# The last sequence's value pages, moved from the end of the paged stage into the prompt's attention

## The chip, the cores and the metric

The kernel runs on one core of one Trainium2 chip. The metric is device microseconds for one execution; the time of the kernel before is the median of three runs. A core has the engines PE (matmul), DVE, ACT and POOL, an SP queue that issues most of the transfers, and 16 DMA engines that move data between HBM and the on-chip memory SBUF. Matmul results land in PSUM.

## What is computed

The reference is one inference step of a trunk of two layers for a prompt of 1024 tokens (with 16 meta tokens ahead of it) and for eight running sequences that each add one token. Layer 0 mixes by gated linear attention, layer 1 by differential attention; each is followed by an MLP and normalisations. The change concerns layer 1. There the prompt attends to itself, and each of the eight new tokens attends to its own 4096 past tokens, whose keys and values lie in 32 pages of 128 tokens, found through a page table:

```python
def diff_core(q, k, v, q_pos, k_pos, lam):
    s = jnp.einsum('bqhmd,bkhmd->bhmqk', q, k).astype(F32) * (DIFF_DH ** -0.5)
    s = jnp.where(k_pos[None, :] <= q_pos[:, None], s, -jnp.inf)
    p = jax.nn.softmax(s, axis=-1)
    a = p[:, :, 0] - lam * p[:, :, 1]
    return jnp.einsum('bhqk,bkhe->bqhe', a, v.astype(F32))
...
    k_past = cache_k[page_table].reshape(B, past, DIFF_HEADS, 2, DIFF_DH)
    v_past = cache_v[page_table].reshape(B, past, DIFF_HEADS, DIFF_DV)
```

All is 32-bit floating point. There are 8 heads; each has two score maps (m = 0, 1), of which the second is subtracted with a learned factor. A page is 128 tokens x 1024 numbers, 512 KB.

## The kernel before, in words

The kernel is one program for one core. The order of instructions on each engine is fixed at build time by a list scheduler, which follows the order of the code and a priority; at run time each engine takes its list in order and waits on semaphores.

The stages that matter here, in order:

**The paged stage.** The generator `decode()` (L855) runs beside layer 0's output, its MLP, and layer 1's projection. For the sequences b = 0 to 7 it loads 32 key pages each, multiplies each with the query (L796, three of four on DVE and one on POOL) and sums per head (L797). `soft()` (L800) makes the softmax weights of a sequence, 33 x 16 numbers on each partition. One sequence later, mixed with the keys of the next, the value pages are loaded (`v_load`, L822) and multiplied (`v_pages`, L832): a page takes four matmuls (L837) with 16 columns of weights each, which write to four groups of partitions of one PSUM bank; all 33 pages (32 and the new token's own value row) add into that bank, `acc`, from the small ring `smt` of two banks. `v_end` (L842) copies the sum out and transposes it to `oT`, which the samples need only in layer 1's output stage. The page loads run in a background priority, behind everything else. In the loop over `range(NS + 1)` the ninth pass has no keys left: it is the eighth sequence's (b = 7) values alone, one page behind the other. Page tiles come from the pool `pgp`, of 8 buffers of 4 KB a partition. A page's load reads its number from the page table into a register on SP (`value_load`), and each such read is issued after the fourth load before it.

**Layer 1's projection** (L1091 on): 12 units of 256 columns, matmuls L186 to L188 with a left operand XH, XL and split weights. A unit's result is copied to a tile `qo` (L1104) and stored (L1121). After unit 8, `prep_qk(0, ...)` prepares head 0 of the attention. After the stage the pools of the paged stage are closed (`de.close()`), and attention's own pools are opened on the right side of SBUF, upon bytes that the closed pools had; a tile waits for the tiles that had its bytes before.

**The prompt's attention** (loop at L1240): 8 heads of 8 tiles of 128 queries. `prep(h)` (L1170) loads a head's keys and queries (L1059, L1060), the meta tokens' keys (L1061), the meta values `vm` (L1175) and the values `vx` (L1176) on SP's queue, transposes keys and queries on PE (L1068 to L1078), splits them in two (L182, L183), and moves halves between partitions by nine transfers on POOL's queue (L1082 to L1088). It is called one head ahead. `tile_` (L1179) makes the scores of a tile on PE (L1192, L1193), brings them to SBUF with mask and running minimum on DVE (L1196), exponentiates on ACT (L1198), combines the two maps on DVE (L1202), transposes on PE (L1211), copies on ACT (L1213) and multiplies with the values on PE (L1216). The products of four tiles gather in one bank `po` from the ring `smt`; then ACT copies them out (L1251) and squares them in place (L1252), and DVE sums the squares (L1253).

After it come layer 1's output matrix (`w_out`), with the samples' part `samples()`, and the second MLP.

Of the kernel before, what the change touches and what calls it, by code (L numbers as in the profile page):

```python
# [11 lines left out]
F32 = mybir.dt.float32  # L12
F32R = mybir.dt.float32r
U8 = mybir.dt.uint8
I32 = mybir.dt.int32
AF = mybir.ActivationFunctionType
ALU = mybir.AluOpType
# [9 lines left out]
NS = 8  # L27
# [83 lines left out]
def hybrid_step(ctx, tc, A, dbg=None, upto=9):  # L111
# [20 lines left out]
    def smt():  # L132
        return sm.tile([P, 512], F32, name="smt")
# [602 lines left out]
    @contextmanager  # L736
    def background():
        at = tc.cur_priority
        tc.cur_priority = bg_at[0]
        yield  # L740
        bg_at[0] = tc.cur_priority
        tc.cur_priority = at

    ptab = dp.tile([NS, NPG], I32, name="ptab")
    dma(ptab, A["page_table"])

    lamv = kp.tile([P, 2], F32, name="lamv")
# [9 lines left out]

    gathers = []

    def page(cache, b, n):  # L760

        with tc.issue_after(gathers[-4]) if len(gathers) > 3 else nullcontext():
            r = nc.sync.value_load(ptab[b : b + 1, n : n + 1], min_val=0, max_val=A["cache_k"].shape[1] - 1)
        t = pgp.tile([P, D], F32, name="pg")
        gathers.append(dma(t, A[cache][0, ds(r, 1)].rearrange("a p h d -> (a p) (h d)")).ins)
        return t

# [13 lines left out]
    def k_start(b):  # L781
        sc = dp2.tile([P, NPG + 1, 16], F32, name="sc")
        qb = dp.tile([P, D], F32, name="qb")
        with background():
            dma(qb, A["qs"][b : b + 1, :].broadcast_to([P, D]))
            V.memset(sc[:, NPG, :], NEG)
            V.tensor_scalar(sc[:NS, NPG, :], own, other[:NS, b : b + 1], None, ALU.add)
        return sc, qb

    def k_page(b, n, sc, qb):  # L790
        with background():
            pg = page("cache_k", b, n)
            eng, after = (G, steps_g) if n % 4 == 3 else (V, steps_v)

            with tc.issue_after(after[-1]) if (b == 0 and n < 24 and after) or (b == HOLD[0] and HOLD[1] <= n) else nullcontext():
                eng.tensor_tensor(pg, pg, qb, op=ALU.mult)  # L796
            return V.tensor_reduce(sc[:, n, :], pg.rearrange("p (h d) -> p h d", d=64), op=ALU.add, axis=AX.X).ins  # L797

    def soft(sc):

        mx = dp.tile([P, 16], F32, name="mx")
        V.tensor_reduce(mx, sc.rearrange("p n c -> p c n"), op=ALU.max, axis=AX.X)
        ps = smt()
        TE.transpose(ps[:16, :P], mx, ident)
        m1 = dp.tile([16, 1], F32, name="m1")
        V.tensor_reduce(m1, ps[:16, :P], op=ALU.max, axis=AX.X)
        ps = smt()
        TE.matmul(ps[:, :16], m1.broadcast_to([16, P]), ident[:16, :16], start=True, stop=True)
        V.tensor_tensor(sc, sc, bc(ps[:, :16], [P, NPG + 1, 16], 1), op=ALU.subtract)
        S.activation(sc, sc, AF.Exp, scale=0.125)  # L810
        V.tensor_reduce(mx, sc.rearrange("p n c -> p c n"), op=ALU.add, axis=AX.X)
        ps = smt()
        TE.matmul(ps[:, :16], one, mx, start=True, stop=True)
        cf = dp.tile([P, 16], F32, name="cf")
        V.reciprocal(cf, ps[:, :16])
        cv = cf.rearrange("p (c m) -> p c m", m=2)
        V.tensor_tensor(cv, cv, bc(lamv, [P, 8, 2], 1), op=ALU.mult)
        V.tensor_tensor(sc, sc, bc(cf, [P, NPG + 1, 16], 1), op=ALU.mult)
        av = sc.rearrange("p n (c m) -> p n c m", m=2)
        V.tensor_tensor(av[:, :, :, 0], av[:, :, :, 0], av[:, :, :, 1], op=ALU.add)  # L820
        return sc

    def v_load(b, n):
        with background():
            if n < NPG:
                return page("cache_v", b, n)
            pg = pgp.tile([P, D], F32, name="pg")
            G.memset(pg[:32], 0.0)
            dma(pg[:NS], A["v_rows_s"][0, :, 0].rearrange("b h d -> b (h d)"))
            return pg  # L830

    def v_pages(pages, w, acc, behind):  # L832

        for n, pg in pages:
            r = slice(0, P if n < NPG else 32)
            for i in range(4):
                m = TE.matmul(acc[i * TS : i * TS + 16, :256], w[r, n, :], pg[r, i * 256 : (i + 1) * 256], start=n == 0, stop=n == NPG).ins  # L837
                if behind is not None:

                    tc.add_manual_dep(m, behind.name, mybir.DependencyInfo(mybir.DependencyClass.NoSync, mybir.DependencyReason.DATA), reason="order")  # L840
                    behind = None

    def v_end(b, acc):

        ev = pgp.tile([P, D], F32, name="pg")[:, :256]
        G.memset(ev, 0.0)
        for i in range(4):
            S.copy(ev[i * TS : i * TS + 16, :], acc[i * TS : i * TS + 16, :256])
        pt = smt()
        for j in range(2):  # L850
            TE.transpose(pt[:, j * P : (j + 1) * P], ev[:, j * P : (j + 1) * P], ident)
        for j in range(2):
            V.tensor_copy(oT[:, j : 8 : 2, b], pt[:, 130 * j : 130 * j + 36 * 3 + 1 : 36])

    def decode():  # L855
        ks = None
        for b in range(NS + 1):
            prev = ks
            if b < NS:
                ks = k_start(b)  # L860
            if b > 0:
                w = soft(prev[0])
                acc = smt()
            held, k = [], None
            for n in range(NPG):
                if b == 0 or (b == HOLD[0] and HOLD[1] <= n < HOLD[1] + 16):
                    yield b
                if b < NS:
                    k = k_page(b, n, *ks)
                if b > 0:  # L870

                    if len(held) == 2:
                        v_pages(held, w, acc, k)
                        held = []
                    held.append((n, v_load(b - 1, n)))
            if b > 0:
                held.append((NPG, v_load(b - 1, NPG)))
                v_pages(held, w, acc, None)
                v_end(b - 1, acc)

    for c in range(2):
        cs = slice(512 * c, 512 * c + 512)
# [161 lines left out]


    e = ExitStack()
    rp = e.enter_context(tc.tile_pool(name="rp", bufs=1))
    qt = e.enter_context(tc.tile_pool(name="qt", bufs=3))
    ht = e.enter_context(tc.tile_pool(name="qht", bufs=2))
# [97 lines left out]
    scp = e.enter_context(tc.tile_pool(name="scp", bufs=5, **own_bytes))  # L1147
    a2 = e.enter_context(tc.tile_pool(name="a2", bufs=4, **own_bytes))
    a3 = e.enter_context(tc.tile_pool(name="a3", bufs=6, **own_bytes))
    Y = cp.tile([P, 8192], F32, name="Y2", tag="Y")  # L1150
    Yt = Y.rearrange("p (t n) -> p t n", n=D)
    CW = 448
# [11 lines left out]
    def prep(h):  # L1164
        kr = A["k_rows_p"][0, 0, :, h, :]
        vr = A["v_rows_p"][0, 0, :, h, :]
        vk = wsp.tile([P, 2048], F32R, name="whi").bitcast(F32)
        vx = vk[:, :1024].rearrange("p (t d) -> p t d", d=P)
        km, vm = vk[:NM, 1024 : 1024 + P], vms[h % 2]
        if h == 0:  # L1170
            parts = head0
        else:
            raw = wsp.tile([P, 2048], F32R, name="wlo").bitcast(F32)
            parts = prep_qk(h, raw, km, *(x.t[h % 2].rearrange("p a n -> p (a n)") for x in (XH, XL)))
        dma(vm[:NM], vr[:NM])  # L1175
        dma(vx, vr[NM:].rearrange("(t p) d -> p t d", p=P))  # L1176
        return vm, vx, *parts

    def tile_(h, t, out, vm, vx, k2, q2, ql2):  # L1179
        W = NM + P * (t + 1)  # L1180
# [56 lines left out]


    nxt = prep(0)
    for h in range(8):  # L1240
        head = nxt
        for n, t in enumerate((3, 2, 1, 0, 7, 6, 5, 4) if h == 7 else (7, 1, 5, 3, 6, 0, 4, 2)):
            if n == 0 and h < 7:
                nxt = prep(h + 1)
            if n % 4 == 0:
                po = smt()
            at = t % 4 if h == 7 else t // 2
            tile_(h, t, po[:, at * P : (at + 1) * P], *head)
            if n % 4 == 3:
                ts = (slice(0, 4), slice(4, 8))[n // 4] if h == 7 else slice(t % 2, 8, 2)  # L1250
                S.copy(Yd[:, ts, h], po.rearrange("p (t e) -> p t e", e=P))  # L1251
                S.activation(po, po, AF.Square)  # L1252
                V.tensor_reduce(oss[:, ts, h], po.rearrange("p (t e) -> p t e", e=P), op=ALU.add, axis=AX.X)  # L1253
            if n == 3 and h == 7:
                o_norm(V, slice(0, 4), slice(7, 8))
                for j in range(8):
                    o_fm(j, 0)
        if h < 6 and h % 2:
            o_norm(G, slice(0, 8), slice(h - 1, h + 1))
        elif h == 6:  # L1260
            o_norm(G, slice(0, 8), slice(6, 7))
    o_norm(V, slice(4, 8), slice(7, 8))
    for j in range(8):
        o_fm(j, 1)
    e.close()

# [317 lines left out]
```

## Time and profile before

| what | value |
|---|---|
| median of 3 runs | 2919.41 us (2919.35 to 2919.67) |
| the profiled execution | 2927.06 us |
| its span in the profile | 2925.3 us |
| PE busy | 2771.6 us (95%) |
| DVE busy | 1862.0 us (64%) |
| POOL busy | 1124.6 us (38%) |
| ACT busy | 1030.3 us (35%) |
| mean DMA rate | 222 GB/s |

The profile is of one execution; the times of its rows are counted in us from the start of the span. A row of a timeline has the start, the duration, the engine, the line of the code, the operation, what is written and read, and in brackets how long the engine had been idle and what ended that. A row of a group has the line, the engine, the operation, shapes and count, then busy us and mean ns, then idle time before. A row of stretches has for each engine the busy us and in brackets how many instructions, then the granted PE clock (1.00 is full), the share of time in which the 16 DMA engines were busy, and GB/s. A busy PE is not PE at its peak, since matmuls overlap. Numbers of buffers are left out of names: `pg` is any page tile, `smt`, `mmt` and `axt` are PSUM banks, XH, XL and YR hold the operands of the heads, and `as` the scores.

### The profile page before, as it was taken

To read this page: it belongs to the slowest core of one execution; us is meant where nothing else is said; L and a number is where in the kernel's file an instruction comes from. 1 tells how busy PE (TensorE), PEld (TensorE's weight loads), DVE (VectorE), ACT (ScalarE), POOL (GpSimd) and SP (SyncE) were. 2 spreads that over 40 slices of the span, in tenths; PEclk is the share of its full clock that TensorE was granted. 3 is DMA by queue.
4 is the path that set the end of the run, shared out by engine and by line. 5 is a ranking of instruction groups with operands and counts; after the bars stand their busy time and mean duration, and the time that the engine had idled before them with its cause. 6 is when DMAs were issued, how large, how long until landed. Compare 5 with 4: busy or idle time off the path is not lost. (4 is left out here: it accounts for less than half of the span.)

```text
span 2925.3 us, 52101 instructions
## 1 busy us (share of the span) xinstructions
PE 2771.6 (95%) x19625; PEld 2259.1 (77%) x19625; DVE 1862.0 (64%) x2982; ACT 1030.3 (35%) x2066; POOL 1124.6 (38%) x876
## 2 busy tenths in 40 slices
PE   8999989999999999999999996888998999999997
PEld 5876658987777777777898893787887889797885
DVE  2564562457877777777667840788637854738377
ACT  3333342151222222122321110776524534335352
POOL 2221112233433334334233330032235766676674
PEclk9999999999999999999999997999999999999998
DMA  7546751514698988988377999264337878796994
GB/s 257 177 161 232 253 189 47 197 56 142 241 350 298 332 307 302 348 315 321 136 262 260 373 329 313 63 139 98 124 109 203 237 224 231 183 294 167 267 239 87
DMA packets 291272, 648.28 MB, mean 222 GB/s; under 512 B 26231, under 2 KB 142013, under 8 KB 279757
## 3 DMA queue, kind: packets, MB, share of 16 engines
q1 hardware_dynamic: 257900, 530.10, 53.3%
q0 software_dynamic: 33120, 114.87, 16.4%
q8 instruction: 154, 2.52, 0.4%
q14 instruction: 98, 0.79, 0.1%
HBM read 584.98 MB, written 44.06 MB: 215 GB/s over the span
## 5 line engine op out<-in xcount | busy, mean ns | idle before, releaser
L174 POOL TENSOR_TENSOR wlo<-raw,whi 128x512 fp32r<-128x512 f32 x256 | 356.6, 1411 | 745.9 <-ACT whi L173 678.0
L187 PE MATMUL mmt<-wlo,XH 128*128 128x256 f32 (+1 forms) x1760 | 525.0, 299 | 1.4 <-POOL wlo L174 1.4
L186 PE MATMUL mmt<-whi,XH 128*128 128x256 f32 (+1 forms) x1760 | 525.4, 300 | 0.0
L186 PE MATMUL mmt<-XH,whi 128*128 128x512 f32 (+1 forms) x1216 | 435.8, 359 | 7.1 <-DVE HL L183 5.5
L188 PE MATMUL mmt<-whi,XL 128*128 128x256 f32 x1536 | 435.2, 285 | 0.0
L188 PE MATMUL mmt<-XH,wlo 128*128 128x512 f32 (+1 forms) x1216 | 432.8, 357 | 0.0
L173 ACT CAST whi<-raw 128x512 fp32r<-128x512 f32 x256 | 153.0, 620 | 594.5 <-PE mmt L188 186.4
L797 DVE TENSOR_REDUCE sc<-pg 128x16 f32<-128x1024 f32 x256 | 309.2, 1213 | 81.5 <-POOL pg L796 78.3
L187 PEld LDWEIGHTS mmt<-wlo,XH 128*128 128x128 f32 x1760 | 333.4, 190 | 25.3 <-issue 13.3
L186 PEld LDWEIGHTS mmt<-whi,XH 128*128 128x128 f32 x1760 | 331.9, 189 | 26.2 <-issue 14.3
L187 PE MATMUL mmt<-XL,whi 128*128 128x512 f32 x768 | 306.3, 399 | 0.0
L796 DVE TENSOR_TENSOR pg<-pg,qb 128x1024 f32<-128x1024 f32 x192 | 257.7, 1348 | 71.7 <-DMA pg<-in_cache_k 51.2
L188 PEld LDWEIGHTS mmt<-whi,XL 128*128 128x128 f32 x1536 | 290.5, 190 | 11.4 <-issue 10.4
L186 PEld LDWEIGHTS mmt<-XH,whi 128*128 128x128 f32 x1216 | 230.0, 189 | 53.2 <-issue 12.6
L796 POOL TENSOR_TENSOR pg<-pg,qb 128x1024 f32<-128x1024 f32 x64 | 158.4, 2476 | 288.8 <-DMA pg<-in_cache_k 195.6
L188 PEld LDWEIGHTS mmt<-XH,wlo 128*128 128x128 f32 x1216 | 229.9, 189 | 37.1 <-issue 5.0
L186 PE MATMUL mmt<-whi,HH 128*128 128x512 f32 x512 | 205.4, 401 | 2.1 <-DVE Y L1021 2.1
L187 PE MATMUL mmt<-wlo,HH 128*128 128x512 f32 x512 | 204.5, 399 | 0.0
L188 PE MATMUL mmt<-whi,HL 128*128 128x512 f32 x512 | 203.8, 398 | 0.0
L187 PEld LDWEIGHTS mmt<-XL,whi 128*128 128x128 f32 x768 | 145.2, 189 | 37.2 <-issue 6.4
L837 PE MATMUL smt<-pg,sc 128*16 128x256 f32 (+1 forms) x2112 | 146.4, 398 | 23.5 <-DMA pg<-in_cache_v 23.1
L1430 POOL TENSOR_TENSOR wlo<-RW,whi 128x512 fp32r<-128x512 f32 x96 | 151.4, 1661 | 40.2 <-ACT whi L1429 40.1
(448 smaller groups left out, 5693.8 us busy)
## 6 DMA issues: line engine op xcount, KB each, us to landing
pg<-in_cache_k SPq DMA_DIRECT2D x256, 512.0 KB, 6.1
pg<-in_cache_v SPq DMA_DIRECT2D x256, 512.0 KB, 5.7
XH<-xc POOLq DMA_DIRECT2D x42, 1032.0 KB, 8.9
raw<-in_mlp_w SPq DMA_DIRECT2D x164, 256.0 KB, 4.9
rw<-in_mlp_w SPq DMA_DIRECT2D x152, 256.0 KB, 6.0
swt<-in_mlp_w SPq DMA_DIRECT2D x32, 1024.0 KB, 5.9
RW<-in_mlp_w POOLq DMA_DIRECT2D x96, 256.0 KB, 7.0
xc<-XH POOLq DMA_DIRECT2D x14, 1032.0 KB, 7.2
```

The source lines that it names most:

```text
L173: S.copy(hi[:, c], raw)
L174: G.tensor_tensor(lo[:, c], raw, hi[:, c].bitcast(F32), op=ALU.subtract)
L186: TE.matmul(ps, ah, bh, start=first, stop=False)
L187: TE.matmul(ps, ah, bl, start=False, stop=False)
L188: TE.matmul(ps, al, bh, start=False, stop=last)
L796: eng.tensor_tensor(pg, pg, qb, op=ALU.mult)
L797: return V.tensor_reduce(sc[:, n, :], pg.rearrange("p (h d) -> p h d", d=64), op=ALU.add, axis=AX.X).ins
L837: m = TE.matmul(acc[i * TS : i * TS + 16, :256], w[r, n, :], pg[r, i * 256 : (i + 1) * 256], start=n == 0, stop=n == NPG).ins
L1430: G.tensor_tensor(lo[:, k, :], t, hi[:, k, :].bitcast(F32), op=ALU.subtract)
```

## The change

The ninth pass of `decode()` is dropped: the generator ends after the eighth sequence's keys and the seventh's values. The weights of the eighth sequence are copied to a tile `w7` of their own. A new generator, `last_values`, loads and multiplies the 33 value tiles of the eighth sequence amid the prompt's attention: one step after each of the tiles 0 to 6 of a head, and a second step after tile 0, so eight pages a head from head 0 on, and the last, with the end, in head 4. Its pages have a pool of three buffers, are loaded two steps ahead, and have no background priority. The matmuls gather eight pages in one PSUM bank (nine in the last); then DVE adds the four groups of partitions to a tile `ev` in SBUF, and the bank is given back to the ring. `v_out` is the second half of the former `v_end`. The page table moves to a pool that stays open. The squares of attention's output are now made from the copied tile in SBUF, into a part of the head's value tile that is not used, `sq`, rather than in place in PSUM.

```diff
-    ptab = dp.tile([NS, NPG], I32, name="ptab")
+    ptab = kp.tile([NS, NPG], I32, name="ptab")
...
-    def page(cache, b, n):
+    def page(cache, b, n, pool=None):
...
-        t = pgp.tile([P, D], F32, name="pg")
+        t = (pool or pgp).tile([P, D], F32, name="pg")
...
-    def v_pages(pages, w, acc, behind):
+    def v_pages(pages, w, acc, behind, begin=(0,), end=(NPG,)):
...
-                m = TE.matmul(acc[i * TS : i * TS + 16, :256], w[r, n, :], pg[r, i * 256 : (i + 1) * 256], start=n == 0, stop=n == NPG).ins
+                m = TE.matmul(acc[i * TS : i * TS + 16, :256], w[r, n, :], pg[r, i * 256 : (i + 1) * 256], start=n in begin, stop=n in end).ins
...
     def decode():
         ks = None
-        for b in range(NS + 1):
+        for b in range(NS):
...
+        V.tensor_copy(w7, soft(ks[0]))
+
+    def last_values(pool, ev):
+
+        G.memset(ev, 0.0)
+        ahead = 2
+        pages = [(n, v_load(NS - 1, n, pool)) for n in range(ahead)]
+        for n in range(NPG + 1):
+            if n % 8 == 0 and n < NPG:
+                acc = smt()
+            if n + ahead <= NPG:
+                pages.append((n + ahead, v_load(NS - 1, n + ahead, pool)))
+            v_pages([pages[n]], w7, acc, None, (0, 8, 16, 24), (7, 15, 23, NPG))
+            if n in (7, 15, 23, NPG):
+                for i in range(4):
+                    r = slice(i * TS, i * TS + 16)
+                    V.tensor_tensor(ev[r], ev[r], acc[r, :256], op=ALU.add)
+            yield n
+        v_out(NS - 1, ev)
...
+    w7e = ExitStack()
+    w7p = w7e.enter_context(tc.tile_pool(name="w7p", bufs=1, side="right"))
+    w7 = w7p.tile([P, NPG + 1, 16], F32, name="w7")
...
+    vp = e.enter_context(tc.tile_pool(name="vp", bufs=3, **own_bytes))
...
+        sq = vk[:, 1536:]
...
+    last = last_values(vp, a1.tile([P, 256], F32, name="ev"))
     for h in range(8):
-        head = nxt
+        sq, *head = nxt
...
             tile_(h, t, po[:, at * P : (at + 1) * P], *head)
+            if n < 7:
+                next(last, None)
+            if n == 0:
+                next(last, None)
             if n % 4 == 3:
                 ts = (slice(0, 4), slice(4, 8))[n // 4] if h == 7 else slice(t % 2, 8, 2)
                 S.copy(Yd[:, ts, h], po.rearrange("p (t e) -> p t e", e=P))
-                S.activation(po, po, AF.Square)
-                V.tensor_reduce(oss[:, ts, h], po.rearrange("p (t e) -> p t e", e=P), op=ALU.add, axis=AX.X)
+                S.activation(sq.rearrange("p (t e) -> p t e", e=P), Yd[:, ts, h], AF.Square)
+                V.tensor_reduce(oss[:, ts, h], sq.rearrange("p (t e) -> p t e", e=P), op=ALU.add, axis=AX.X)
```

More of the change, by code (lines that the diff above doesn't have):

```diff
@@ L821, in soft, with v_load @@
         return sc
[L823 to L830, printed above, removed]
-    def v_pages(pages, w, acc, behind):
+    def v_load(b, n, pool=None):
+        if n < NPG:
+            return page("cache_v", b, n, pool)
+        pg = (pool or pgp).tile([P, D], F32, name="pg")
+        G.memset(pg[:32], 0.0)
+        dma(pg[:NS], A["v_rows_s"][0, :, 0].rearrange("b h d -> b (h d)"))
+        return pg
+    def v_pages(pages, w, acc, behind, begin=(0,), end=(NPG,)):
         for n, pg in pages:
@@ L848, in v_end, with v_out @@
             S.copy(ev[i * TS : i * TS + 16, :], acc[i * TS : i * TS + 16, :256])
+        v_out(b, ev)
+    def v_out(b, ev):
         pt = smt()
@@ L856, in decode @@
         ks = None
-        for b in range(NS + 1):
+        for b in range(NS):
             prev = ks
-            if b < NS:
-                ks = k_start(b)
+            ks = k_start(b)
             if b > 0:
@@ L867, in decode @@
                     yield b
-                if b < NS:
-                    k = k_page(b, n, *ks)
+                k = k_page(b, n, *ks)
                 if b > 0:
@@ L874, in decode @@
                         held = []
-                    held.append((n, v_load(b - 1, n)))
+                    with background():
+                        held.append((n, v_load(b - 1, n)))
             if b > 0:
-                held.append((NPG, v_load(b - 1, NPG)))
+                with background():
+                    held.append((NPG, v_load(b - 1, NPG)))
                 v_pages(held, w, acc, None)
                 v_end(b - 1, acc)
+        V.tensor_copy(w7, soft(ks[0]))
[15 more added lines that the diff above has]
+        v_out(NS - 1, ev)
     for c in range(2):
@@ L1176, in prep @@
         dma(vx, vr[NM:].rearrange("(t p) d -> p t d", p=P))
-        return vm, vx, *parts
+        return sq, vm, vx, *parts
     def tile_(h, t, out, vm, vx, k2, q2, ql2):
@@ L1265, in hybrid_step @@
     e.close()
+    w7e.close()
     e = ExitStack()
```

## The prediction

> **What bounds the kernel now.** I read first the table of stretches (busy time of each engine between two times, then granted clock, share and rate of the DMA engines), cut where the chain of work changes hands. The heads of the prompt's attention are told apart by the issues of the small load of a head's meta values (line 1175), which comes when a head's last product is done.
>
> ```profile
> core 0: us, PE busy (x) PEld busy (x) DVE busy (x) ACT busy (x) POOL busy (x), PEclk, DMA share, GB/s
> 1756.30:1782.10 25.80, 25.39 (x242) 20.36 (x240) 3.78 (x9) 3.54 (x6) 1.27 (x1) 1.00 0.96 349
> 1782.10:1831.80 49.70, 24.00 (x197) 6.05 (x195) 3.00 (x8) 3.87 (x9) 5.91 (x11) 0.56 0.96 271
> 1831.80:1862.90 31.10, 29.35 (x203) 27.07 (x204) 28.04 (x103) 23.35 (x57) 0.00 (x0) 0.93 0.00 1
> 1862.90:1895.80 32.90, 28.16 (x201) 25.40 (x200) 24.52 (x84) 21.67 (x50) 4.58 (x9) 0.95 0.60 121
> 1895.80:1923.80 28.00, 25.60 (x199) 23.78 (x199) 24.15 (x80) 21.74 (x54) 11.15 (x11) 1.00 0.69 143
> 1923.80:1959.00 35.20, 30.61 (x217) 27.89 (x217) 28.22 (x102) 25.09 (x62) 4.59 (x9) 0.95 0.53 114
> ```
>
> Row 2 is the hole. Before it the projection keeps PE full; after it heads 0 to 3 keep PE, DVE and ACT busy together, with no single bound. In the hole DVE and ACT do almost nothing, the clock falls to 0.56, and only the DMA engines are full (0.96). The same table for the value-page matmuls (line 837) alone, and PE's timeline, say what the hole consists of:
>
> ```profile
> 1756.30:1782.10 25.80, 5.91 (x88) 1.95 (x88) 1.00 0.96 349
> 1782.10:1831.80 49.70, 20.20 (x176) 3.57 (x176) 0.56 0.96 271
> ```
> ```profile
> 1781.72 0.42 PE L1192 MATMUL mmt<-YR 128*128 128x336 f32 x1
> 1782.22 2.35 PE L837 MATMUL smt<-pg,sc 128*16 128x256 f32 x40
> ...
> 1797.34 1.05 PE L837 MATMUL smt<-pg,sc 128*16 128x256 f32 x8 [2.39 <-DMA pg<-in_cache_v]
> 1800.97 1.06 PE L837 MATMUL smt<-pg,sc 128*16 128x256 f32 x8 [2.57 <-DMA pg<-in_cache_v]
> ...
> 1816.30 1.05 PE L837 MATMUL smt<-pg,sc 128*16 128x256 f32 x8 [0.18 <-DMA pg<-in_cache_v]
> ...
> 1821.20 1.06 PE L837 MATMUL smt<-pg,sc 128*16 128x256 f32 x8 [0.17 <-DMA pg<-in_cache_v]
> ...
> 1832.37 0.66 PE L1192 MATMUL mmt<-YR 128*128 128x352 f32 x1 [1.45 <-DVE ast L1196]
> ```
> ```profile
> 1831.78 0.53 DVE L1196 CUSTOM_DVE_ANT_0 as<-mmt,cmask 128x352 f32<-128x352 f32 x1 [0.59 <-issue]
> ```
>
> One page leaves 8 records. 88 + 176 = 264 records are 33 pages: all of the eighth sequence's values, 11 before the hole and 22 in it. Attention's first scores are on PE by 1782.1, but DVE takes them only at 1831.78, after the last page and its evacuation: the score buffers lie on the bytes of the page pool. So 49.7 us of the span are a DMA-bound tail that attention waits for.
>
> **The change part by part.** *Removed, the hole:* with the page tiles of sequence 7 gone, the last users of the old pools are sequence 6's sum, which by the order of the code ends ahead of sequence 7's first page, and the weights of sequence 7, which move to w7. Attention's DVE work can then start when its scores are there: −49.7 us. *Removed ahead of the hole:* 11 pages on a PE with 25.39 of 25.80 us busy: −5.9 us. Together −55.6.
>
> *Kept from the hole:* the preparation of head 1 stood there for free, and now runs beside tile 0 of head 0.
>
> ```profile
> L183 DVE TENSOR_TENSOR XL<-axt,XH 128x512 fp32r<-128x512 f32 (+1 forms) x5 | 2.8, 583 | 24.5 <-ACT XH L182 24.5
> L182 ACT CAST XH<-axt 128x512 fp32r<-128x512 f32 (+1 forms) x5 | 2.4, 504 | 7.9 <-PE axt L1068 6.6 <-PE axt L1078 0.8 <-PE axt L1073 0.4
> L1078 PE MATMUL axt<-c_ident,wlo 128*128 128x128 f32 x8 | 1.7, 354 | 0.3 <-DVE XL L183 0.3
> L1073 PE MATMUL axt<-c_ident,wlo 128*128 128x128 f32 x8 | 1.5, 311 | 0.0
> ```
>
> PE 3.2, DVE 2.8 us: 0 to 3.2 on the path, I take +2. Against it stands that head 0 no longer begins at half clock (0.93 over head 0's 31.1 us is 2.2 us at most): I take −1.
>
> *Added, page matmuls:* 5.91 us / 11 = 0.54 us a page, 33 pages = 17.7 us of PE in heads 0 to 3 (eight pages each; the last in head 4). PE's gaps there are 1.75 + 4.74 + 2.40 + 4.59 = 13.5 us by the four rows above. If pages fell into all of them, 4.2 us would be left; if into none, 17.7. The gaps come from waits that stay and PE takes its list in order, so I take +14.
>
> *Added, adds:* four sums of four 16x256 adds from PSUM, 16 DVE instructions; none exists before. Nearest rows, an ACT copy of this shape and a DVE add of this width on 128 partitions:
>
> ```profile
> L848 ACT COPY pg<-smt x32: 358/363/367, 883.2 to 1829.8; 16x256 f32<-16x256 f32 x32
> ```
> ```profile
> L1472 DVE TENSOR_TENSOR HF<-HF,mmt x64: 407/420/424, 2213.4 to 2816.8; 128x258 f32<-128x258 f32 x64
> ```
>
> 16 x 0.42 = 6.7 us on a DVE that is 82% busy in heads 0 to 3 (104.9 of 127.2 us): 0 to 6.7, I take +3. The four ACT copies of v_end (1.5 us) go with the hole; the closing two transposes and two copies cost under 1 us in head 4 and are in this term.
>
> *PSUM:* the two smt banks served two half-head outputs in turn; now a page sum takes one bank, so the second half of a head waits until the first is copied out, and the next head's first half until four adds are done. The squares now read the copied SBUF tile, so that the bank is free after the copy; same number and size, and I cost that at 0 (ACT and DVE have 0.59 and 0.69 us for it now, the 16 pairs may move by a tenth either way, ±2).
>
> ```profile
> L1251 ACT COPY Y<-smt 128x512 f32<-128x512 f32 x15 | 8.7, 577 | 2.7 <-PE smt L1216 2.7
> ```
>
> Per head 0.58 + 4 x 0.42 = 2.3 us can be exposed, four heads 9 us; scores of later tiles stand between on PE's list and cover most: 0 to 9, I take +2.
>
> *Moved, transfers:* 33 loads of 512 KB go from SP's queue in the hole to SP's queue amid attention. At full rate a page takes (1821.20 − 1816.30) / 4 = 1.23 us; eight per head are 9.8 us of DMA time in some 32 us, beside shares of 0.00, 0.60, 0.69 and 0.53. There is room on average, but not in the bursts in which the next head is prepared, and these are near the path. In the chain in order of time, and on POOL's queue with a burst amid pages (the first pair) and one alone (the second):
>
> ```profile
> 1874.17 9.32 DMA XL<-XL
> ...
> 1884.01 3.28 DMA XL<-XL
> ...
> 1936.23 9.54 DMA XL<-XL
> ```
> ```profile
> 1789.97 0.56 POOL L1082 DMA_DIRECT2D XH<-XH  x1 [31.78 <-ACT XH L182]
> ...
> 1797.46 0.52 POOL L1083 DMA_DIRECT2D XH<-XL  x1 [4.03 <-DMA XH<-XH]
> ...
> 1869.87 0.51 POOL L1082 DMA_DIRECT2D XH<-XH  x1 [50.90 <-ACT XH L182]
> ...
> 1876.49 0.51 POOL L1083 DMA_DIRECT2D XH<-XL  x1 [1.81 <-DMA XH<-XH]
> ```
>
> A burst runs from 1869.87 to 1884.01 + 3.28 = 1887.3, 17.4 us. It would meet 9.8 x 17.4 / 32 = 5.3 us of page transfers. Lines 1082 to 1083 took 7.5 us amid eight waiting pages and 6.6 alone, so the moves suffered by 0.9 us there. Three bursts (heads 2, 3, 4) lie among pages: 0 to 16 us, near the second pair I take 3 x 2 = +6. The Trainium skill, DMA: Bandwidth & Descriptors, section Queues, rings and completion order, says that each DMA engine takes turns, packet by packet, between the queues that have work. By that rule the moves on POOL's queue would run at half speed for as long as pages wait on SP's, an estimate nearer the 16 than the 6; the pair of rows shows less.
>
> Sum: −55.6 + 2 − 1 + 14 + 3 + 2 + 6 = **−29.6 us**. The profiled execution took 2927.06 us around its span of 2925.3 and gives 2897.5; it stands 7.65 us (0.26%) above the median, which gives 2919.41 − 29.6 = **2889.8**, rounded to 2890.
>
> **Rivals.** *All hidden (chance 0.13):* pages fill PE's gaps, transfers and adds cost nothing: −55.6 + 4.2 − 1 = −52.4, 2867. For it: 13.5 us of gaps; against: those gaps are tied to bursts and DVE. *The bursts bind (0.17):* 16 us in place of 6, and the pages' matmuls wholly on the path (17.7 for 14): −15.9, 2903.5. For it: the chain already goes through the moves at 1874 and 1936. *The start stays late (0.06):* scores wait for something else beneath their bytes, such as the output tiles of the last projection, whose store leaves only at the projection's end; it would land some 6 us (5.7 for a page, below) after: 2896, the change doing most of what it says, and up to 2919 if pages still hold the pool.
>
> *Slower (0.06):* SP takes its list in order, and the load of line 1175 waits there for PE.
>
> ```profile
> SPq L1175 <- PE smt L1216: 70.3, 2, 45.3
> ```
> ```profile
> pg<-in_cache_v SPq DMA_DIRECT2D x256, 512.0 KB, 5.7
> ```
>
> Loads of pages behind it, and behind buffers (three, with two pages ahead), start late; PE, in order too, then waits at a page matmul for 5.7 us, and twice for a next page at the pace of 1797.34 to 1800.97, 3.6 us: 13 us a head, 52 in four heads, 2942. It decides from 29.6 / 4 = 7.4 us a head. Against it: a load is issued about three tiles (31.1 / 8 = 3.9 us each) before its use, 11.7 us, and 3.6 us a page is still under a tile.
>
> **How the numbers follow.** The forecast, with 0.58, has its own range 2880 to 2900. All terms at their good ends give −54 or so (2866), all at the bad ends −55.6 + 3.2 + 17.7 + 6.7 + 2 + 9 + 16 = −1 (2918); 2873 to 2907 takes in the bursts and leaves out about a tenth on either side. This kernel's measurement tells about 0.2% (5.8 us) from no change. Faster: all but the slower rival and the ends of two others: 0.92; same 0.03; slower 0.05.
>
> **What would show it.** Right: no stretch without DVE work between the projection and head 0, the first line-1196 work within some 3 us of the last projection matmul; the first score matmul's work about 55 us earlier; heads 0 to 3 longer by 5 to 7 us each; clock near 1.0 throughout; 8 page records each in heads 0 to 3 at 0.54 us a page. The burst term is right if the moves' waits grow by some 2 us a head, wrong if PE shows waits for XH or XL of 5 us. Long waits of PE for pg would show the slower rival. Wrong altogether: the first line-1196 work still behind a page or a store, or a changed order of PE's work in the projection that takes back what the pages gave.

## The result and the profile after

| | median us | range, runs | ratio to before, 95% interval |
|---|---|---|---|
| before | 2919.78 | 2914.97 to 2926.20, 12 | |
| after | 2923.16 | 2917.34 to 2928.43, 12 | 1.0007 [0.9998, 1.0017] |

No difference that this measurement can tell, against a forecast of −29.6 us. The hole closed as forecast, and nearly all of the lead was given back in heads 0 to 3. The profiled execution of the changed kernel took 2917.34 us around a span of 2915.6. That is 5.8 us under its median, and the profiled execution of the kernel before is 7 us above its own; so differences of rows between these two profiles carry some 13 us of scatter, and the sizes below rest on medians. Line numbers have moved: scores are now L1222 (were L1196), `vm` L1201 (L1175), the meta tokens' keys `km` L1085 (L1061), page matmuls L836 (L837).

The stretches of the changed kernel, cut at the issues of `vm` as in the prediction (the first row starts 2.6 us after the first score work); the rows are heads 0 to 5, with the same columns:

```profile
1776.40:1817.30 40.90, 35.72 (x267) 26.82 (x267) 29.30 (x104) 23.79 (x56) 4.64 (x9) 0.99 0.74 187
1817.30:1857.50 40.20, 33.48 (x255) 24.91 (x254) 23.29 (x74) 20.48 (x49) 4.58 (x9) 0.96 0.79 196
1857.50:1909.30 51.80, 41.75 (x287) 32.66 (x286) 35.11 (x111) 26.07 (x60) 12.22 (x11) 0.87 0.66 165
1909.30:1954.20 44.90, 34.70 (x263) 26.14 (x263) 22.93 (x75) 21.39 (x51) 5.52 (x10) 0.89 0.68 149
1954.20:1991.10 36.90, 31.93 (x219) 29.38 (x219) 31.74 (x106) 25.36 (x58) 11.18 (x11) 0.91 0.49 108
1991.10:2022.80 31.70, 29.35 (x205) 27.22 (x204) 25.92 (x85) 23.07 (x55) 4.58 (x9) 0.89 0.40 93
```

PE's last matmul of the projection in the kernel before; then, in the changed kernel, the same, the first score matmul, the first transpose of head 1's preparation, and DVE's work up to the first scores:

```profile
1779.78 0.38 PE L188 MATMUL mmt<-whi,XL 128*128 128x256 f32 x1
```
```profile
1768.41 0.28 PE L188 MATMUL mmt<-whi,XL 128*128 128x256 f32 x1
1768.53 0.33 PE L1218 MATMUL mmt<-YR 128*128 128x352 f32 x1
...
1773.15 0.23 PE L1092 MATMUL axt<-c_ident,whi 16*128 16x16 f32 x1 [3.16 <-DMA whi<-out_k_rows_p]
```
```profile
1773.62 0.17 DVE L183 TENSOR_TENSOR XL<-axt,XH 128x16 fp32r<-128x16 f32 x1 [14.56 <-ACT XH L182]
...
1773.85 0.53 DVE L1222 CUSTOM_DVE_ANT_0 as<-mmt,cmask 128x352 f32<-128x352 f32 x1
```

Attention starts 1831.78 − 1773.85 = 57.9 us earlier, and the gap between projection and first score work falls from 51.6 to 5.2 us. The 5.2 that stay have a reason: scores are on PE from 1768.53, but DVE's fixed list has the split of head 1's first piece (L183) ahead of them, and that waits for the load of head 1's `km`, which is issued at the projection's end. The chain of work that ended last has this load:

```profile
1769.08 4.02 DMA whi<-out_k_rows_p
```

Before, that wait stood in the hole (2.57 us of PE at 1787.15). Head 3 ends at 1954.20, and ended at 1959.00 before: the lead is down to 4.8 us. By the rows heads 0 to 3 take 177.8 us in place of 127.2, 12.7 more each, where the forecast had 5 to 7. Of these 50.6 us more, PE is idle for 18.7 (32.2 in place of 13.5) and busy for 31.9. The page matmuls make 24.3 of the latter, by the same table for line 836 alone (264 records, the 33 pages, where the forecast had 17.7); the rest is the same attention work, at a clock of 0.87 and 0.89 in heads 2 and 3, where it was 1.00 and 0.95.

Two things stand out. The first is on SP's queue. Rows of its timeline in the changed kernel (start, duration, issue); `vm` is issued when a head's last product is done, and `km` of the head after next stands behind it:

```profile
1817.26 0.34 SPq L1201 DMA_DIRECT2D vm<-out_v_rows_p  x1
1822.40 0.34 SPq L1085 DMA_DIRECT2D whi<-out_k_rows_p  x1
...
1832.23 23.43 SPq L765 DMA_DIRECT2D pg<-in_cache_v  x8
1857.49 0.34 SPq L1201 DMA_DIRECT2D vm<-out_v_rows_p  x1
1862.14 0.33 SPq L1085 DMA_DIRECT2D whi<-out_k_rows_p  x1
```

SP's waits after (1770 to 2100 us), then those of the kernel before (1832 to 2100 us); the columns are us in total, times, the longest:

```profile
SPq L1085 <- DVE oss L1284: 26.8, 6, 5.4
```
```profile
SPq L1061 <- PE mmt L1193: 2.9, 5, 0.6
```

Before, `km` left 0.7 us behind `vm`. Now it leaves 5 us behind, and it waits for `oss`, the sum of squares. The reason is in one line of the diff: `sq = vk[:, 1536:]` writes the squares into the unused end of the head's value tile. `km` of the head after next reuses that tile's buffer, and the buffer is free only when its last reader is done; that was the last product on PE, and is now DVE's last sum.

The second is on PE. Its timeline at the turn to head 1, and POOL's over the same stretch (the moves that prepare head 2):

```profile
1831.55 1.47 PE L836 MATMUL smt<-pg,w 128*16 128x256 f32 x18
1832.95 0.55 PE L1237 MATMUL axt<-c_ident,as 128*128 128x128 f32 x3
1833.42 0.61 PE L836 MATMUL smt<-pg,w 128*16 128x256 f32 x4
1833.97 1.38 PE L1242 MATMUL smt<-whi,aT 128*128 128x128 f32 x10
1835.28 0.60 PE L836 MATMUL smt<-pg,w 128*16 128x256 f32 x2
...
1842.83 0.62 PE L836 MATMUL smt<-pg,w 128*16 128x256 f32 x8 [2.36 <-DMA pg<-in_cache_v]
...
1845.88 0.61 PE L836 MATMUL smt<-pg,w 128*16 128x256 f32 x4 [0.95 <-DMA pg<-in_cache_v]
```
```profile
1829.47 0.51 POOL L1106 DMA_DIRECT2D XH<-XH  x1 [36.54 <-ACT XH L182]
...
1831.97 0.54 POOL L1111 DMA_DIRECT2D XL<-XL  x1
```

A page leaves eight records, so 18 + 4 + 2 are three pages: PE's fixed list has them close together, and empties all three buffers within 4.3 us. The next loads leave from 1832.23 on, amid the moves of the burst, and PE stands at the pages that follow. The chain of work that ended last goes through such a load in each of heads 0 to 3 (start, us), and the matmuls wait 17.2 us for pages between 1765 and 1975 us, their weight loads 19.6, much of it the same time:

```profile
1790.26 9.73 DMA pg<-in_cache_v
...
1832.84 13.00 DMA pg<-in_cache_v
...
1877.65 10.30 DMA pg<-in_cache_v
...
1926.60 18.48 DMA pg<-in_cache_v
```
```profile
PEld smt L836 <- DMA pg<-in_cache_v: 19.6, 9, 6.3
...
PE smt L836 <- DMA pg<-in_cache_v: 17.2, 8, 6.1
```

### The profile page after: what moved, and what is told of

Its sections match the earlier page's. It is cut to its first block, busy times and chain, and to the rows that moved or that the text cites. A ratio compares the mean times of both kernels' runs of the same rounds, so it can differ in the third digit from the quotient of the medians.

```text
span 2915.6 us, 52092 instructions
## 1 busy us (share of the span) xinstructions
PE 2774.7 (95%) x19625; PEld 2262.5 (78%) x19625; DVE 1867.6 (64%) x2999; ACT 1031.8 (35%) x2062; POOL 1128.7 (39%) x876
## 4 chain that ended last, share of the span: by engine, by line
PE 66%; DMA 10%; DVE 10%; issue 3%; POOL 2%; ACT 1%; SPq 0%; DVEq 0%; POOLq 0%; ACTq 0%
PE mmt L186 15%; PE mmt L187 15%; PE mmt L188 15%; PE smt L836 4%; PE axt L186 2%; PE axt L188 2%; PE axt L187 2%; PE smt L1242 2%; DMA XH<-xc 2%; DMA pg<-in_cache_v 2%; DVE as L1222 1%; DVE pg L796 1%; PE axt L1237 1%; DMA raw<-in_mlp_w 1%; POOL wlo L1462 1%
## 5 line engine op out<-in xcount | busy, mean ns | idle before, releaser
L187 PEld LDWEIGHTS mmt<-wlo,XH 128*128 128x128 f32 x1760 | 332.3, 189 | 25.6 <-issue 13.7
L796 DVE TENSOR_TENSOR pg<-pg,qb 128x1024 f32<-128x1024 f32 x192 | 258.3, 1351 | 68.3 <-DMA pg<-in_cache_k 46.4
L1462 POOL TENSOR_TENSOR wlo<-rw,whi 128x512 fp32r<-128x512 f32 x92 | 143.6, 1626 | 37.5 <-ACT whi L1461 34.7
```

Source lines behind the costliest of these rows:

```text
L187: TE.matmul(ps, ah, bl, start=False, stop=False)
L1462: G.tensor_tensor(lo[:, k, :], t, hi[:, k, :].bitcast(F32), op=ALU.subtract)
```

## The experiments

Times are medians; "before" is the kernel before, measured beside the run. All differences are under 2%. Runs e1, e2, e3, e6 and e12 leave out the values of the eighth sequence's pages; the others are complete. The theory at the outset was that late pages on a PE in fixed order ate the gain; the rivals were that the transfers slow the moves, that the added work costs more than forecast, and that the hole was worth less.

| run | what it is | us | before | difference | ratio, 95% |
|---|---|---|---|---|---|
| e1_none | after, without the 32 pages | 2890.69 | 2919.74 | −29.1 | 0.9905 [0.9884, 0.9926] |
| e2_mm_only | after, matmuls without loads | 2902.75 | 2919.74 | −17.0 | 0.9943 [0.9921, 0.9964] |
| e3_unawaited | e2 and the loads, awaited by nobody | 2902.58 | 2919.74 | −17.2 | 0.9942 [0.9922, 0.9962] |
| e4_order | after, pages queued behind their tile on PE | 2906.16 | 2919.74 | −13.6 | 0.9956 [0.9944, 0.9968] |
| e5_before_sq | before, squares in the value tile | 2940.64 | 2917.97 | +22.7 | 1.0075 [1.0052, 1.0098] |
| e6_none_own | e1, squares in a tile of their own | 2872.53 | 2917.97 | −45.4 | 0.9851 [0.9824, 0.9878] |
| e7_after_own | after, squares in a tile of their own | 2905.90 | 2917.97 | −12.1 | 0.9954 [0.9939, 0.9970] |
| e8_order_own | e4 and e7 together | 2897.85 | 2917.97 | −20.1 | 0.9927 [0.9903, 0.9951] |
| e9_best | e8, four pages a head in all eight heads | 2904.23 | 2919.77 | −15.5 | 0.9947 [0.9931, 0.9963] |
| e10_spread_own | e9 without the order on PE | 2910.02 | 2919.77 | −9.8 | 0.9970 [0.9955, 0.9986] |
| e11_order_psum | e4, squares in place in PSUM as before | 2905.58 | 2919.77 | −14.2 | 0.9956 [0.9939, 0.9972] |
| e12_before_none | before, without the 32 pages | 2873.44 | 2920.95 | −47.5 | 0.9842 [0.9816, 0.9869] |

**What the pages cost, taken apart: e1 to e3.** e1 leaves out loads and matmuls, e2 multiplies resident zeros, e3 does so too and issues the loads at the pace of the change.

```diff
-        for n in range(NPG + 1):
...
+        for n in range(NPG, NPG + 1):
```

That is e1; e2 is the first two lines of this, e3 all of it, with a load held back until the matmuls of the page before are done:

```diff
-            v_pages([pages[n]], w7, acc, None, (0, 8, 16, 24), (7, 15, 23, NPG))
+            v_pages([(n, None)], w7, acc, None, (0, 8, 16, 24), (7, 15, 23, NPG))
...
-                pages.append((n + ahead, v_load(NS - 1, n + ahead, pool)))
+                v_load(NS - 1, n + ahead, pool)
```

> Leaves out the 32 value pages of the eighth sequence, loads and matmuls both; its own new value row, one sum and the closing transposes stay, in head 0. It tells what the hole is worth when nothing is put into attention. All theories that blame the added work in attention expect about 2865 us (2858 to 2872), that is 55 us under before, as the forecast had it. Near 2900 or above, the hole was worth less than its 55 us, and the gain was never there to be lost.

> All 33 x 4 page matmuls and the sums in attention, but on zeros that lie in SBUF: no page of the eighth sequence is loaded (its values are left out). Theory of the wait (PE, in order, stands at a page matmul whose load lands late): 10 to 20 us above the run without pages, about 2880. Rival, the work itself (PE's 18 us, 16 adds, the PSUM ring of two banks that ties page sums to half-head outputs): near the changed kernel, 2910 to 2925.

> The loads are issued as in the changed kernel, each behind the matmuls of the page three before it, and the matmuls stand where they stood, but read zeros in SBUF, so PE never waits for a load (values left out). Theory of the wait: within 10 us of the matmuls alone, 2880 to 2892. Rival, the bursts (page transfers slow the moves and loads that prepare the next head): most of the loss stays, 2905 to 2923.

Measured: −29.1, −17.0, −17.2. In absolute times all three lie between the ranges that the theories gave. Against each other they go as the theory of the wait has it: e2 is 12 us above e1 (10 to 20 expected), and e3 beside e2 (within 10). The work of the pages is 12 us. For their transfers no cost is seen beside it: e3 and e2 differ by 0.2, where each median is known to some 6 us. That the loads are awaited costs about 20.6 (2923.16 − 2902.58), with one reserve: the scheduler makes a list for each run, and the lists of e2 and e3 are not the very list of the change. And something is missing that has nothing to do with pages: without any, the program is only 29 us faster, not 55. POOL's waits for its moves between 1770 and 1975 us, e2 first, then e3:

```profile
POOL XH L1108 <- DMA XH<-XH: 22.5, 5, 6.1
POOL XH L1103 <- DMA XH<-XH: 12.2, 4, 5.8
POOL XL L1108 <- DMA XL<-XL: 11.7, 5, 3.6
```
```profile
POOL XH L1118 <- DMA XH<-XH: 26.2, 5, 8.0
POOL XL L1118 <- DMA XL<-XL: 17.4, 4, 5.4
POOL XH L1113 <- DMA XH<-XH: 4.2, 2, 2.7
```

46.4 us of waiting without page transfers, 47.8 with them. The moves themselves landed in a median of 8.1 (XH<-XH), 9.5 (XL<-XL) and 8.8 us (XH<-XL) in e2, and in 8.2, 10.0 and 9.4 in e3, by the rows of DMA issues from 1770 to 1960 us: the bursts don't bind. By the turns that the Trainium skill describes (DMA: Bandwidth & Descriptors, section Queues, rings and completion order) the estimate for moves beside waiting pages was about half speed; these rows don't show it.

**The order on PE: e4.** A page's matmuls are queued behind the last product of the tile they follow in the code, with no wait on a semaphore.

```diff
-            TE.matmul(out, at, v, start=j == 0, stop=j == t + 1)
+            tile_end[:] = [TE.matmul(out, at, v, start=j == 0, stop=j == t + 1).ins]
...
-            v_pages([pages[n]], w7, acc, None, (0, 8, 16, 24), (7, 15, 23, NPG))
+            v_pages([pages[n]], w7, acc, tile_end[0], (0, 8, 16, 24), (7, 15, 23, NPG))
```

> The changed kernel, with each page's matmuls queued on PE behind the last product of the tile that they follow in the code, so that at most one page (two after a head's first tile) falls into a tile's time and a load has about three tiles to land. Theory of the wait, with the bunching of page matmuls early in a head as its cause: 2890 to 2908. If the wait comes from the late issue of the loads alone (behind the next head's loads on SP's queue), or from the bursts, little changes: 2915 to 2925.

Measured: −13.6, 17 us better than the change, whose interval it doesn't touch, with the same work, transfers and buffers. So the order of the pages in PE's list is worth 17 us. Taking away the wait (e3, whose list is bunched too) or the order (e4, whose loads are awaited) gives back nearly the same, so the loss comes from the two together. How it comes about is less clear. PE's waits for pages, 17.2 us in the change, are in e4 (1770 to 2090 us):

```profile
PE smt L837 <- DMA pg<-in_cache_v: 12.1, 4, 5.0
```

That is 5 us less, not 17. And at the turn to head 1 PE takes three pages within 2.5 us in e4 too (16 records from 1830.31, 8 from 1832.22), and stands 4.83 us at the fourth. So emptied buffers are a part of it at most; the place of the pages among the products of the tiles may have a price of its own. Ordered matmuls on zeros (e2 with this edit) would tell, and were not run.

**The squares' tile: e5 to e7.** e5 does this one edit on the kernel before; e6 and e7 take it out of e1 and of the change.

```diff
+        sq = vk[:, 1536:]
...
-                S.activation(po, po, AF.Square)
+                S.activation(sq.rearrange("p (t e) -> p t e", e=P), Yd[:, ts, h], AF.Square)
```

This is e5, with the sum reading `sq`; the next is e6 and e7:

```diff
+    sq = a1.tile([P, 512], F32, name="sqo")
...
-        sq = vk[:, 1536:]
```

> The kernel before with only one part of the change: the squares of a half head go from the copied tile into the unused end of that head's value tile instead of in place in PSUM. Theory of the lent tile (the value tile is given back only after the last sum of squares, so the small key load behind which the preparation of the head after next stands leaves 3 to 6 us later in each head): slower by 10 to 22 us, 2930 to 2942. The forecast's own cost of this edit was 0 within 2: 2918 to 2922.

> No value pages of the eighth sequence (as in the run without pages), and the squares in an SBUF tile of their own. Theory of the lent tile: the missing part of the hole's worth comes back, 2865 to 2873, 18 to 26 us under the run without pages. Rival (the hole also hid the preparation of head 1 and gave the heads a start that is now gone): it stays near 2885 to 2891.

> The changed kernel with the squares in an SBUF tile of their own, pages as they are. If the lent tile and the waits for pages add up: 2900 to 2908. If the waits for pages take the place of the delayed preparation (both lie in the first half of a head): 2915 to 2923, no change.

Measured: the edit alone costs the kernel before 22.7 us; with a tile of its own instead, e1 gains 16 us (29.1 to 45.4) and the change 15.5. SP's waits for the buffer in e5, where the line is L1061, and in e6, where it is L1082 (both 1770 to 2075 us):

```profile
SPq L1061 <- DVE oss L1254: 33.0, 6, 6.3
```
```profile
SPq L1082 <- PE mmt L1216: 3.1, 6, 0.6
```

The wait comes with the edit and goes with it, and in these runs so does the time. The instructions themselves cost what they cost before (before, then after):

```profile
L1253 DVE TENSOR_REDUCE oss<-smt 128x4 f32<-128x512 f32 x16 | 11.0, 686 | 0.0
L1252 ACT ACTIVATE smt<-smt 128x512 f32<-128x512 f32 x16 | 9.4, 589 | 0.1
```
```profile
L1284 DVE TENSOR_REDUCE oss<-whi 128x4 f32<-128x512 f32 x16 | 10.9, 681 | 0.4 <-ACT whi L1283 0.3
...
L1283 ACT ACTIVATE whi<-Y 128x512 f32<-128x512 f32 x16 | 10.1, 632 | 0.1
```

**Both mended: e8.** The edits of e4 and e7 in one kernel.

> Page matmuls queued behind the tile that they follow, and squares in a tile of their own: both causes taken away. If they add up: 2884 to 2893, which is the forecast's 2890. If the heads are bound otherwise by then: 2900 to 2906.

Measured: −20.1, the lowest median of the versions that are complete, and 0.7% under the kernel before. It lies between the two ranges, so the causes add up only in part. Order and tile overlap: either gives 15.5 to 17 us first, and the other then 6.5 to 8 more, by medians whose intervals (e4 and e8, e7 and e8) overlap. PE still stands at pages for a while, by its waits (1770 to 2090 us):

```profile
PE smt L837 <- DMA pg<-in_cache_v: 12.0, 3, 6.4
```

**Spread over eight heads: e9, e10.** A page after every second tile, four to a sum.

```diff
-            if n < 7:
-                next(last, None)
-            if n == 0:
-                next(last, None)
+            if n % 2 == 0:
+                next(last)
...
-            if n % 8 == 0 and n < NPG:
+            if n % 4 == 0 and n < NPG:
```

> Page matmuls behind their tile, squares in a tile of their own, and pages spread over all eight heads: one page after every second tile, four a head in eight sums of four, the last five at the end of head 7. A load then has some six tiles to land. Theory of the wait: PE's remaining 12 us of waits for pages go, less some work that now falls in the later heads: 2882 to 2892, 6 to 15 us under the run with eight pages a head. If those waits were only in the place of other waits: 2895 to 2901.

> As the run before it in this call, but the page matmuls are not queued behind their tile. If three buffers and half the rate are slack enough: within 4 us of it. If the scheduler's early placing is what makes PE wait, whatever the rate: 5 to 12 us above it.

Measured: e9 −15.5, no better than e8 (the intervals overlap), and e10 −9.8. The expectation for e9 was missed. e10 is 5.8 us above e9, as its second branch has it, though the intervals overlap; PE waits 13.7 us for pages there (1770 to 2090 us), at half the rate. PE's list of waits in e9 has none for a page any more, but DVE has a new one; its waits for page sums (1770 to 2090 us) in e8, then in e9:

```profile
DVE ev L899 <- PE smt L837: 1.5, 2, 1.0
```
```profile
DVE ev L899 <- PE smt L837: 20.1, 7, 11.8
```

DVE, in fixed order as well, now stands at its adds until PE has come to the pages: a wait moved from one engine to the other, and there are eight sums in place of four. That this wait is what ate the gain was read from the profile, and not tried by itself.

**The bank: e11.** e4, with the squares in place in PSUM as before, so that the bank is held through the squares and their sum.

```diff
-                S.activation(sq.rearrange("p (t e) -> p t e", e=P), Yd[:, ts, h], AF.Square)
+                S.activation(po, po, AF.Square)
```

> Eight pages a head behind their tiles, and the squares in place in PSUM as in the kernel before, so that an output bank is held through copy, squares and sum of squares (two more instructions, 0.59 + 0.69 us, and their queues). The forecast's PSUM term (0 to 9 us, taken as 2, with the bank given back after the copy) says 0 to 9 above the run with a tile of its own, 2898 to 2907. Theory of the lent tile needs it under the run with the squares in the value tile, 2906, or at most beside it.

Measured: −14.2, some 6 us behind e8, with intervals that overlap: holding the bank costs at most about what the forecast gave as its bound. It is also within 0.6 us of e4, which has the lent tile in place of the held bank. SP's waits for `oss` (1770 to 2075 us) are 23.6 us in e4, and there are none in e11, yet the time is the same. So once the pages are in order the lent tile costs no more than the bank, 6 us or so, and its 15 to 23 us hold for programs without that order.

**The hole by itself: e12.** The kernel before with nothing changed but that the eighth sequence's pages are left out.

```diff
-            for n in range(NPG):
+            for n in range(NPG if b < NS else 0):
```

> The kernel before with the 32 value pages of the eighth sequence left out, loads and matmuls (the new token's own value row stays): the hole closed with nothing of the change in it, neither the three page buffers, the tile w7, the four sums nor the squares in another place. Closing the hole in the changed program, with the squares in a tile of their own, brought -45.4 us where the forecast had -54.6. Theory 'the hole gave a head start' (it let head 1 be prepared and head 2 be loaded while the pages came in): it is lost here too, about -45 us, 2870 to 2878. Rival 'the changed program carries 10 us of its own' (pool order, w7, page table): not here, -55 us, 2860 to 2866. Within head 1 and 2 the first theory expects some 3 us a head more than the 32.9 and 28.0 us of before.

Measured: −47.5, with no part of the change in it. That agrees with e6: the hole was worth 45 to 48 us, though the interval (−54 to −38) nearly reaches the forecast's 54.6. The number is the one that the first theory gave, and the rival's −55 (the changed program carries 10 us of its own) lies just outside the interval. Its stretches, heads 0 to 3:

```profile
1770.90:1803.50 32.60, 30.67 (x212) 28.56 (x211) 29.12 (x103) 24.89 (x59) 4.66 (x9) 0.92 0.62 135
1803.50:1836.50 33.00, 28.33 (x205) 26.30 (x204) 25.73 (x85) 21.76 (x53) 4.61 (x9) 0.95 0.56 121
1836.50:1872.40 35.90, 29.90 (x197) 27.30 (x196) 28.12 (x78) 21.71 (x53) 11.21 (x11) 0.86 0.52 111
1872.40:1910.00 37.60, 34.12 (x229) 30.74 (x229) 32.16 (x115) 27.32 (x65) 4.59 (x9) 0.91 0.50 107
```

Head 0 now moves data (DMA share 0.62 where it was 0.00): head 1's moves and head 2's loads, which the hole had done. But heads 0 and 1 are 1.5 and 0.1 us longer than before, and heads 2 and 3 7.9 and 2.4, so the place that the expectation named (3 us each in heads 1 and 2) is wrong. Two parts can be read in the trace. The start waits for head 1's `km` load here too, 4.6 us behind the projection (1766.36 to 1770.92). And in head 2 (the third row) PE stands 4.69 us at one instruction of DVE, a combine that runs while POOL issues moves and multiplies Y (the rows are DVE's, POOL's and PE's):

```profile
1849.43 6.30 DVE L1202 SCALAR_TENSOR_TENSOR as<-as,ast 128x784 f32<-128x784 f32 x1
```
```profile
1851.26 3.63 POOL L1228 TENSOR_TENSOR Y<-Y,orr 128x2048 f32<-128x2048 f32 x1
```
```profile
1855.88 0.45 PE L1211 MATMUL axt<-c_ident,as 128*128 128x128 f32 x1 [4.69 <-DVE as L1202]
```

The kernel before has a combine of this shape in its head 2 at 1.03 us. This second part is no lost head start, but a meeting of two engines that depends on when each comes to its instruction. The size of the loss is measured; how it divides between a lost head start and such meetings is not.

## Why the prediction was wrong, point by point

**The hole (−49.7) and the 11 pages ahead of it (−5.9).** The mechanism was right: the start came 57.9 us earlier, where some 55 were forecast, though 5.2 us behind the projection and not 3. The rival of a late start falls. As a gain it was 9 us too large: with +2 for head 1's preparation and −1 for the clock the forecast had −54.6, and e6 gives −45.4. The failing step is "the preparation of head 1 stood there for free", with +2. It priced the instructions of the preparation, and not the load that they wait for: DVE has them ahead of the first scores, so the start stands 4.6 to 5.2 us behind the projection (e12 and the change). The rest of the 9 us is open; the stall of 4.69 us in e12's head 2 is one candidate.

**The squares: the step that failed first.** "Same number and size, and I cost that at 0." The instructions did cost 0 (0.7 us in 16 pairs on ACT, nothing on DVE). But the edit made the value tile live longer, and its buffer is what the next preparation's first transfer waits for. That is 22.7 us alone on the kernel before, 15.5 in the change against a tile of its own, and 6.5 once the pages are in order (e4 − e8 by their differences). The prediction counted the instructions of the edit and the bank that it frees, and not the buffer that it holds.

**Page loads: the step that failed second.** The slower rival had the right mechanism: loads behind others on SP, three buffers, a PE that takes its list in order and stands at a page. It was given 0.06 and 52 us; it happened at 20.6 us (after − e3). Against it stood "a load is issued about three tiles before its use". That took the order of the code, one page per tile, for the order on PE: the list scheduler put pages close together and ahead of products that they follow in the code, and e4, which forbids the latter, has back 17 us. PE's listed waits for pages fell by only 5 of these, so that the order counts is shown, and that it counts through emptied buffers is in part argued. The forecast of 5 to 7 us a head was exceeded for that reason and for the squares, 12.7.

**Page matmuls (+14), adds (+3), PSUM (+2).** e2 − e1 has them together at 12 us, under the forecast's 19 and inside its bounds (both runs have the lent tile). The adds were sized right:

```profile
L898 DVE TENSOR_TENSOR ev<-ev,smt 16x256 f32<-16x256 f32 x16 | 6.7, 416 | 3.6 <-PE smt L836 3.4
```

16 of them at 0.416 us, where the forecast took 0.42 from a wider add. With order and tile mended, e8 − e6 is 25.3 us, the very sum of these terms with the bursts (14 + 3 + 2 + 6 = 25), but by chance: by e2 − e1 and PE's waits it is about 12 of work and 12 in which PE waits for pages.

**Bursts (+6), and the rival in which they bind.** −0.2 by e3 − e2, which the scatter of the two medians (some 6 us each) leaves open between nothing and a few us; the rival's 16 is out. That the moves landed only 0.1 to 0.6 us later beside pages speaks for nearly nothing. The average space that the prediction saw on the DMA engines was enough.

**The clock** was 0.87 to 0.99 in heads 0 to 3, not near 1.0 throughout; the runs don't tell what that is worth.

The sum then stands so: −54.6 forecast for the hole with its terms, +9.2 for what it brought beside, +25.3 for work and waits for pages that remain in e8, +8.0 for the order on PE with the tile mended (e7 − e8), +15.5 for the lent tile, together +3.4 us. That it closes is no proof, since each term is a difference of two runs' results. The last two overlap and can be split the other way, 17.0 and 6.5. Open is what a fourth page buffer would save of the 12 us of waits for pages that are left in e8; it wasn't tried.

## What to carry to other kernels

When an edit reads or writes a tile in a new place, ask first which buffer now lives longer and who waits for it, and only then what the instruction costs: here the instruction was free, and its buffer cost 22.7 us on the kernel before. Work that is inserted "one piece per step" in the code is spread only if the list of the engine is: read the timeline of that engine, for here the order alone was worth 17 us. And a hole in the profile can be worth less than its length: here 45 to 48 us of 55.6, since work that waited inside it, such as a load for the next head, has to wait somewhere else.

## What the runs showed of the hardware that was not expected

Thirty-two loads of 512 KB, laid beside a stage whose chain runs through other transfers, cost no time that these runs can tell as long as nobody waited for them: 2902.58 us against 2902.75 without, each known to some 6 us. The loads' own time from issue to landing varied between the runs, and not with the order on PE: by the rows of DMA issues from 1770 to 1960 us the median is 7.2 us in the change and 7.7 in e4, which has the order; it is 8.1 in e7 and 6.0 in e8, which has it too. The kernel before had 5.7 over its whole span.

A combine on DVE (L1202) that met POOL's multiplication of Y (L1228) ended only behind it. In e12 it took 6.30 us, where a combine of that shape took 1.03 in the kernel before, and it ended 0.8 us after POOL. In the kernel before two of 528 columns took 4.75 and 5.02 us in the same position, ending 0.6 us after POOL, where one apart from such work took 0.76. Scores on DVE (L1196) beside the same multiplication took 0.31 to 0.55 us as elsewhere (1909.74, 1910.50 and 1911.80 in the kernel before). Why the one is held and the other is not wasn't tried.
